# A hybrid decoder layer on one core: cross-attention begun beside its queries, MLP operands by column halves, and the next head's values differenced in a fixed place

## The chip, the core and the metric

The kernel runs on one core of a Trainium2 chip. Five engines work beside each other, each through its own instructions in order: TensorE (PE: matmuls and transposes into PSUM), VectorE (DVE), ScalarE (ACT), GpSimd (POOL) and SyncE (SP, here only issuing DMAs). The metric is the device time in microseconds of one launch.

## The reference

One layer on x of 1024 tokens by 1024 columns, all in float32: a state-space part and stick-breaking attention side by side, an output projection, cross-attention to 256 memory tokens, and an MLP with squared ReLU; then a last RMSNorm. Cut to what the change touches:

```
def stick_breaking_attention(q, k, v):      # 8 heads of 64
    logits = q @ k.T / 8,  mask: s < t
    later = cumsum(log_sigmoid(-logits), from the right) - own
    out[t] = sum_s exp(log_sigmoid(logits) + later)[t, s] * v[s]

def memory_cross_attention(hn, mem, ...):   # 4 heads of 128, 256 memory tokens
    p = softmax(q @ k.T / sqrt(128));  return (p @ v) @ w_o

def sqrelu_mlp(hn, w1, w2):                 # 1024 -> 4096 -> 1024
    return square(relu(hn @ w1)) @ w2

h = x + hybrid_mixer(rmsnorm(x));  h = h + memory_cross_attention(rmsnorm(h), rmsnorm(mem))
h = h + sqrelu_mlp(rmsnorm(h));    out = rmsnorm(h)
```

## The kernel before

Every matmul of float32 operands is done as three (lines 208 to 210), on an upper part (`whi`, rounded by ScalarE) and the rest (`wlo`, a subtraction of VectorE); the helpers `act` (line 107) and `tt` (line 110) record most of ScalarE's and VectorE's work, so the traces are read by tile names. A scheduler orders each engine's instructions by the program's order, by shifts of priority (`later`) and by its own estimates of when an operand is there; the order is then fixed, and each engine waits in it.

**Attention** (`attention`, 230 to 515 us). Per head the values v are loaded twice, shifted by one row (line 710, GpSimd's queue), and their difference is taken on VectorE (`v1`), split and used as the right-hand side of the weighted sum: the sum over s of weights times v is taken over differences of v, so that the running products (the scan of line 739) serve as weights. Per pair of query blocks, m = 0 to 3: logits z (line 736), a sigmoid on ScalarE into `stay`, the scan on VectorE, transposes on TensorE (wT, line 756), the split (wTh, wTl) and the sum into `ops` (line 770). Between them stand matmuls of the projections of the queries and keys (`qkps`; divided by a row factor `rbc` on VectorE) and of the values as filler. The loads and differences of v stand at the head's start, and where the scheduler puts them.

**Cross-attention** (578 to 675 us). `xq(th, a)` makes the queries of head a for half th of the tokens (24 matmuls, `xqps`). `cross` is a unit of one head and one half in two steps: logits `lp`, their maximum and exponentials (`pb`, divided on GpSimd), and then transposes `pT`, their parts `ph` and `pl`, and the sum `avx` with the memory's values. The units are worked one ahead: first step of unit i, second step of unit i-1. Among them stand the last xq and the first four halves of the output product (`xo_half`, `xops`, tables XQ and XF).

**Output and MLP operands** (672 to 732 us). `xo_half(t, n)` makes 512 of the 1024 columns of token tile t (12 matmuls, 2.8 us) and adds them to h on VectorE; `hn` is h times the gain (GpSimd). `rows_T` transposes hn into PSUM (`hT4`, four transposes, line 256, two banks in turn). The MLP's first product is done by a scheme of seven products for a 2 by 2 block, with operands B11, B21 (tokens 0 to 511), B22 and the combinations T1 to T4, each in two parts: with b the transposed half, T1 from t1 = b12 - b11, T2 from t2 = b22 - t1, T3 from t3 = b22 - b12, T4 from r1 = t2 - b21. Before, per token tile, both halves are made and added (`xo_rows`, `gain_rows`) and one tile later transposed and combined (`normB`). VectorE takes the lower part of an operand; `PL` names two operations that GpSimd takes. The first products P1 and P2 of two blocks stand at the end of it, then P6 and P7 begin the MLP proper.

The lines that a scheme can't say, the differences of v in the loop over heads and the order of the units:

```
            tt(v1, v0, v1, ALU.subtract)
            stt(v0[:, 1::2], v0[:, 1::2], B.nlast, v1[:, 1::2], ALU.mult, ALU.add)
...
    for i in range(9):
        for d in range(2):
            if 0 <= i - d < 8:
                next(units[i - d], None)
```

Of the kernel before, what the change touches and what calls it, by code (L numbers as in the profile page):

```python
# [9 lines left out]
F32 = mybir.dt.float32  # L10
# [6 lines left out]
P = 128  # L17
D = 1024
S = 1024
# [4 lines left out]
FF = 4096  # L24
NPR = FF // P // 2
GRP = 8
PL = ('T1', 'R1')
NLAST = 3
E0 = 180
NAHEAD = 2  # L30
# [15 lines left out]
OB = 1  # L46
KKB = 6

XF = (4, 5, 6, 8)
HA0 = 0  # L50
HA1 = 1
LA = 1
# [39 lines left out]
def hybrid_trunk(ctx: ExitStack, tc: tile.TileContext, xT, x, cols, rows, gain, fing, wzd, wp, out):  # L92
# [16 lines left out]
    def tt(out, a, b, op, eng=None):  # L109
        (eng or nc.vector).tensor_tensor(out=out, in0=a, in1=b, op=op)  # L110
# [59 lines left out]
    def split(hi, lo, src):  # L170
        act(hi, src)
        tt(lo, src, hi.bitcast(F32), ALU.subtract)
# [480 lines left out]
    def need(h):  # L653

        ends = {f: 8.0 * (n + 1) for n, f in enumerate(late)}
        return max(ends.get(("qk", h // 2), 0.0), ends.get(("v", h // 4), 0.0), float(N0) if h == 0 else 0.0)
# [41 lines left out]
    nl_ = [0]  # L698

    def attention(heads, B, need=lambda h: 0):  # L700
        for h in heads:
            yield ("need", need(h))
            hh = h % 2

            v0, v1 = (B.p.tile([P, NT, 64], F32, tag=n_, bufs=1, name=n_) for n_ in ("v0", "v1"))
            for o, v in ((1, v0), (0, v1)):
                nc.gpsimd.dma_start(out=v, in_=vd[o:o + S].rearrange("(t p) c -> p t c", p=P)[:, :, 64 * h:64 * h + 64])  # L710
            vt, vl = B.t("vt", [P, NT, P], 2), B.t("vl", [P, 4, P], 2)
            tt(v1, v0, v1, ALU.subtract)
            stt(v0[:, 1::2], v0[:, 1::2], B.nlast, v1[:, 1::2], ALU.mult, ALU.add)
            split(vt[:, :, 0:64], vt[:, :, 64:P], v1)
            split(vl[:, :, 0:64], vl[:, :, 64:P], v0[:, 1::2])
            qs = B.t("qs", [P, S], 2)
            nc.gpsimd.dma_start(out=qs, in_=qd[h])
            ks = []
            for j in range(2):
                ks.append([None, None])  # L720
            for c in range(2):
                for j in range(2):
                    ks[j][c] = B.t("kk", [P, 512], KKB)
                    nc.gpsimd.dma_start(out=ks[j][c], in_=kd[h, 64 * j:64 * j + 128, 512 * c:512 * c + 512])
            opss = {}
            for m in range(4):
                wb = []
                for i in (2 * m, 2 * m + 1):
# [13 lines left out]
                    wb.append(stay)  # L742
                if m % 2 == 0:
                    opss[m // 2] = psum("m1", OB, "ops")
                ops = opss[m // 2]
                oc = 256 * (m % 2)
                for s2_ in range(m + 1):
                    t4 = tr_ps("wT")
                    last = s2_ == m
                    for sb in range(2):  # L750
                        for ii in range(2):
                            if last and sb == 1 and ii == 0:
                                continue
                            o = sb * 256 + ii * P
                            b = 2 * s2_ + sb
                            nc.tensor.transpose(out=t4[:, o:o + P], in_=wb[ii][:, b * P:(b + 1) * P], identity=ident)  # L756
                    with later(-WP):
                        if last:
                            wh, wl = B.wlast[nl_[0] % len(B.wlast)]
                            nl_[0] += 1  # L760
                            for sl in (slice(0, 256), slice(384, 512)):
                                split(wh[:, sl], wl[:, sl], t4[:, sl])
                        else:
                            wh = B.wT("wTh")
                            wl = B.wT("wTl")
                            split(wh, wl, t4)
                    for sb in range(2):
                        v = vl[:, m, :] if last and sb == 1 else vt[:, 2 * s2_ + sb, :]
                        for j, w in enumerate((wh, wl)):
                            nc.tensor.matmul(out=ops[:, oc:oc + 256], lhsT=v, rhs=w[:, sb * 256:sb * 256 + 256],  # L770
                                             start=(s2_ == 0 and sb == 0 and j == 0), stop=(last and sb == 1 and j == 1))
                if m % 2 == 1:
                    od = oT[64 * hh:64 * hh + 64, h // 2, 512 * (m // 2):512 * (m // 2) + 512]
                    act(od, ops[64:128, :], scale=-1.0)
                    tt(od, od, ops[0:64, :], ALU.subtract)
                yield (3.0 + 4.0 * m) / 36.0

    bctx = ExitStack()
# [82 lines left out]
    def calloc(shape, dt, name):  # L861
        return cpl.tile(shape, dt, tag="c", bufs=NC, name=name)
# [123 lines left out]
            mm3(ps, (vm[0][:, mb, a * P:(a + 1) * P], vm[1][:, mb, a * P:(a + 1) * P]), (ph, pl), mb == 0, mb == 1)  # L986
        split(xo[th][:, 0, a, :], xo[th][:, 1, a, :], ps)

    for th in range(2):
        for a in range(2):  # L990
            xq(th, a)
            if th == 0 and a == TL:
                for t in range(NT - LAG1, NT):
                    turn(t)

    xq(0, 2)
    xq(0, 3)
# [15 lines left out]
        ns = slice(512 * n, 512 * n + 512)  # L1013
        tt(h[t][:, ns], ps, h[t][:, ns], ALU.add)

    units = [cross(th, a) for th in range(2) for a in range(4)]
    for i in range(9):
        for d in range(2):
            if 0 <= i - d < 8:
                next(units[i - d], None)  # L1020
        if i in XQ:
            xq(1, 2 + XQ.index(i))
        if i in XF:
            if not wxo:
                wxo.extend(pieces("xo", 0, 4))
            xo_half(XF.index(i), 0)
# [20 lines left out]
    gff = cpl.tile([P, D], F32, name="gff")  # L1047
    nc.scalar.dma_start(out=gff, in_=gain.partition_broadcast(P))

    def gain_rows(t):  # L1050

        hns[t] = []
        for kh in range(2):
            hn = calloc([P, 512], F32, "hn")
            sl = slice(512 * kh, 512 * kh + 512)
            tt(hn, h[t][:, sl], gff[:, sl], ALU.mult, nc.gpsimd)
            hns[t].append(hn)
        nc.sync.dma_start(out=hd[t * P:(t + 1) * P, :], in_=h[t])

    hns = {}  # L1060

    def normB(t):

        th, o = t // 4, (t % 4) * P
        K4 = [P, 4, P]
        for kh in range(2):
            b = rows_T(hns[t][kh])
            if th == 0:
                act(raw[:, kh, :, o:o + P], b)
                splitB(("B11", "B21")[kh], o, b)  # L1070
            elif kh == 0:
                b12, t1 = calloc(K4, F32, "b12"), calloc(K4, F32, "t1")
                tt(t1, b, raw[:, 0, :, o:o + P], ALU.subtract)
                act(b12, b)
                splitB("T1", o, t1)
            else:
                t2, t3 = (calloc(K4, F32, n_) for n_ in ("t2", "t3"))
                tt(t2, b, t1, ALU.subtract)
                tt(t3, b, b12, ALU.subtract)
                splitB("B22", o, b)  # L1080
                r1 = raw[:, 1, :, o:o + P]
                tt(r1, t2, r1, ALU.subtract, nc.gpsimd if "R1" in PL else None)
                splitB("T2", o, t2)
                splitB("T3", o, t3)

    wxo.extend(pieces("xo", len(wxo), 6 - len(wxo)) + pieces("xo", 6, 2, (xop, "woh", "wol", 2)))

    def xo_rows(t):
        for n in range(2):
            xo_half(t, n)  # L1090

    for t in range(4 + LAG):
        xo_rows(t)
        gain_rows(t)
        if t >= LAG:
            normB(t - LAG)
    B["T2"] = hp.tile([P, 2, 4, 512], F32R, tag="h0", name="T2")
    B["T3"] = big(0, [P, 2, 4, 512], F32R, "T3")
    for t in range(4 + LAG, NT):
        xo_rows(t)  # L1100
        gain_rows(t)
        normB(t - LAG)
    for t in range(NT - LAG, NT):
        normB(t)
    B["T4"] = big(1, [P, 2, 4, 512], F32R, "T4")
    for o in range(0, 512, P):
        r1 = raw[:, 1, :, o:o + P]
# [342 lines left out]
```

## Time and profile before

| | |
|---|---|
| median of 3 runs | 1359.4 us (1359.32 to 1359.65) |
| the profiled execution | 1360.99 us, its span 1359.3 us |
| granted TensorE clock, mean | 0.993 |
| weight loads (beside the matmuls) | 1063.8 us, 78% |
| SyncE's queue of DMAs | 155.78 MB, 36.3% of 16 DMA engines |

The profiled execution took 1.6 us more than the median, and its span is 1.7 us shorter than its own time. A granted clock of 1 is 2.4 GHz, 0.5 is 1.2 GHz. Busy times of TensorE hold short waits inside a pipelined row of matmuls, so its idle time is read where it stands ahead of an instruction, in brackets with what released it.

### The profile page before, as it was taken

What the parts mean: (1) busy time and instruction counts of PE and PEld (TensorE: products, weight loads), DVE (VectorE), ACT (ScalarE), POOL (GpSimd) and SP (SyncE); (2) the same over time, 40 slices, a digit from 0 to 9 for tenths busy, and PEclk for the clock granted to TensorE, in tenths of its full rate; (3) what the DMA queues carried; (4) which work ended last, traced back from release to release, by engine and by line L of the source; (5) the groups of instructions that cost most, each with busy time, mean ns of one, the idle gap of its engine ahead of it and who ended that gap; (6) DMA issues with size and microseconds to landing.
All of it is one profiled execution on the core that took longest, in us unless ns stands there. A gap on an engine that the chain in (4) does not pass through costs nothing.

```text
span 1359.3 us, 18383 instructions
## 1 busy us (share of the span) xinstructions
PE 1307.3 (96%) x6469; PEld 1063.8 (78%) x6469; DVE 942.6 (69%) x1523; ACT 701.4 (52%) x1341; POOL 204.3 (15%) x232
## 2 busy tenths in 40 slices
PE   9999999889999899999998999999999999999997
PEld 7989977678767778887786888888887788888885
DVE  7757865586789856546569756665667866589685
ACT  7455542465567633556445545444553585444453
POOL 0000001310211001003363333223330000000000
PEclk9999999899999999999999999999999999999998
DMA  6111345752556524121133554445449943633341
GB/s 219 40 63 47 102 135 138 222 156 67 159 146 203 149 92 132 31 63 32 59 113 124 186 163 138 142 155 163 140 145 331 300 152 93 231 95 95 98 156 70
DMA packets 95852, 181.68 MB, mean 134 GB/s; under 512 B 9808, under 2 KB 14992, under 8 KB 95760
## 3 DMA queue, kind: packets, MB, share of 16 engines
q1 hardware_dynamic: 85040, 155.78, 36.3%
q0 software_dynamic: 8624, 18.88, 5.1%
q10 hardware_dynamic: 2096, 5.84, 1.2%
q8 instruction: 51, 0.84, 0.3%
q14 instruction: 41, 0.34, 0.1%
HBM read 128.00 MB, written 52.46 MB: 133 GB/s over the span
## 4 chain that ended last, share of the span: by engine, by line
PE 78%; DVE 8%; issue 6%; ACT 3%; DMA 3%; POOL 1%; SPq 0%; POOLq 0%; ACTq 0%; DVEq 0%
PE P L208 7%; PE P L210 7%; PE P L209 7%; PE pr L208 7%; PE pr L209 7%; PE pr L210 7%; DVE stay L739 4%; PE o L210 2%; PE o L208 2%; PE o L209 2%; PE ops L770 1%; PE wT L756 1%; DMA wst<-in_wp 1%; PE qkps L208 1%; PE qkps L210 1%
## 5 line engine op out<-in xcount | busy, mean ns | idle before, releaser
L208 PE MATMUL pr<-whi 128*128 128x512 f32 x448 | 175.9, 396 | 3.5 <-ACT whi L107 3.5
L209 PE MATMUL pr<-wlo,whi 128*128 128x512 f32 x448 | 176.8, 395 | 0.2 <-DVE wlo L110 0.2
L210 PE MATMUL pr<-whi,wlo 128*128 128x512 f32 x448 | 176.2, 393 | 0.0
L110 POOL TENSOR_TENSOR c<-c 128x512 f32<-128x512 f32 x60 | 87.1, 1462 | 202.1 <-ACT c L107 199.7
L110 DVE TENSOR_TENSOR wlo<-w1r,whi 128x512 fp32r<-128x512 f32 x92 | 76.9, 838 | 44.3 <-ACT whi L107 44.3
L107 ACT ACTIVATE whi<-w1r 128x512 fp32r<-128x512 f32 x92 | 57.8, 630 | 92.9 <-PE P L209 52.0
L208 PEld LDWEIGHTS pr<-whi 128*128 128x128 f32 x448 | 83.9, 188 | 24.9 <-ACT whi L107 4.4
L208 PE MATMUL P<-T,whi 128*128 128x512 f32 x256 | 101.0, 395 | 0.9 <-ACT p L107 0.6
L210 PE MATMUL P<-T,wlo 128*128 128x512 f32 x256 | 100.7, 394 | 0.0
L209 PE MATMUL P<-T,whi 128*128 128x512 f32 x256 | 100.6, 393 | 0.0
L209 PEld LDWEIGHTS pr<-wlo,whi 128*128 128x128 f32 x448 | 84.2, 188 | 20.4 <-DVE wlo L110 1.2
L210 PEld LDWEIGHTS pr<-whi,wlo 128*128 128x128 f32 x448 | 84.1, 188 | 20.2
L107 ACT ACTIVATE c<-c 128x512 f32<-128x512 f32 x132 | 81.6, 628 | 24.7 <-DVE c L110 23.1
L107 ACT ACTIVATE whi<-wst 128x512 fp32r<-128x512 f32 (+1 forms) x88 | 54.2, 629 | 67.4 <-PE o L210 24.9
L739 DVE TENSOR_TENSOR_SCAN stay<-stay,dg 128x128 f32<-128x128 f32 (+3 forms) x64 | 84.8, 1346 | 3.9 <-ACT stay L107 3.8
L107 ACT ACTIVATE whi<-us 128x512 fp32r<-128x512 f32 x64 | 40.3, 630 | 79.9 <-PE pr L209 67.0
L210 PE MATMUL P<-B,wlo 128*128 128x512 f32 x192 | 76.3, 397 | 0.0
L208 PE MATMUL P<-B,whi 128*128 128x512 f32 x192 | 76.2, 397 | 0.0
L209 PE MATMUL P<-B,whi 128*128 128x512 f32 x192 | 76.1, 396 | 0.0
L110 DVE TENSOR_TENSOR wlo<-wst,whi 128x512 fp32r<-128x512 f32 (+1 forms) x88 | 61.8, 718 | 19.6 <-ACT whi L107 18.3
L110 DVE TENSOR_TENSOR wlo<-us,whi 128x512 fp32r<-128x512 f32 x64 | 44.9, 701 | 34.1 <-ACT whi L107 33.5
L756 PE MATMUL wT<-ident,stay 128*128 128x128 f32 x288 | 51.3, 282 | 16.5 <-DVE stay L739 15.0
(341 smaller groups left out, 3411.1 us busy)
## 6 DMA issues: line engine op xcount, KB each, us to landing
ud<-c SPq DMA_DIRECT2D x112, 256.0 KB, 3.3
wst<-in_wp SPq DMA_DIRECT2D x104, 256.0 KB, 2.8
w1r<-in_wp SPq DMA_DIRECT2D x16, 1024.0 KB, 6.4
us<-ud SPq DMA_DIRECT2D x64, 256.0 KB, 2.7
pair<-in_wp SPq DMA_DIRECT2D x16, 1024.0 KB, 7.7
kk<-kd POOLq DMA_DIRECT2D x32, 256.0 KB, 5.2
p<-ud SPq DMA_DIRECT2D x24, 256.0 KB, 2.6
u<-ud SPq DMA_DIRECT2D x24, 256.0 KB, 2.6
```

The lines of the kernel that those rows point to most:

```text
L107: nc.scalar.activation(out=out, in_=in_, func=func, **kw)
L110: (eng or nc.vector).tensor_tensor(out=out, in0=a, in1=b, op=op)
L208: nc.tensor.matmul(out=ps, lhsT=a[0], rhs=b[0], start=start, stop=False)
L209: nc.tensor.matmul(out=ps, lhsT=a[0], rhs=b[1], start=False, stop=False)
L210: nc.tensor.matmul(out=ps, lhsT=a[1], rhs=b[0], start=False, stop=stop)
L739: nc.vector.tensor_tensor_scan(out=stay[:, 0:W][:, ::-1], data0=stay[:, 0:W][:, ::-1], data1=B.dg1[:, S - W:S][:, ::-1], initial=0.0, op0= ...
L756: nc.tensor.transpose(out=t4[:, o:o + P], in_=wb[ii][:, b * P:(b + 1) * P], identity=ident)
L770: nc.tensor.matmul(out=ops[:, oc:oc + 256], lhsT=v, rhs=w[:, sb * 256:sb * 256 + 256], start=(s2_ == 0 and sb == 0 and j == 0), stop=(last ...
```

## The change

Three parts, in the code and then in the engines' orders. In `attention` the loads of head h+1's values are issued in the second query pair (m == 1) of head h, and the differences are taken in the third (m == 2), with the first of them kept at its place in the program's order; only heads 0 and 7 do both themselves, freely placed. In the cross-attention the first steps of units 0 and 1 stand between the first xq, and the loop runs two units ahead. In the output stage the work goes by column halves: all eight token tiles of columns 0 to 511, then all of 512 to 1023, one half behind; `PL` is empty, so VectorE takes T1's lower part, and t2 is now t3 + b11 from SBUF instead of b22 - t1 from PSUM (r1 stays on GpSimd). XF moves one of the four early output halves by one unit, all weights of xo go through one ring, and h is stored once per token tile when its second half is done.

```diff
-PL = ('T1', 'R1')
+PL = ()
-XF = (4, 5, 6, 8)
+XF = (4, 5, 6, 7)
...
+        def differ_v(h, pinned=True):
+            v0, v1 = vts[h]
             vt, vl = B.t("vt", [P, NT, P], 2), B.t("vl", [P, 4, P], 2)
-            tt(v1, v0, v1, ALU.subtract)
+            ins = nc.vector.tensor_tensor(out=v1, in0=v0, in1=v1, op=ALU.subtract)
+            if pinned:
+                tc.keep_in_program_order(ins)
...
+                if h + 1 in heads:
+                    if m == 1:
+                        yield ("need", need(h + 1))
+                        load_v(h + 1)
+                    elif m == 2:
+                        differ_v(h + 1)
...
+    xq(0, 1)
+    next(units[0])
+    xq(1, 0)
+    next(units[1])
+    xq(1, 1)
...
-    for i in range(9):
-        for d in range(2):
-            if 0 <= i - d < 8:
-                next(units[i - d], None)
+    for i in range(8):
+        next(units[i], None)
+        if i + 2 < 8:
+            next(units[i + 2])
...
+        elif n == 0:
+            b12s[t], t1 = xop.tile(K4, F32, tag="b12", bufs=4, name="b12"), calloc(K4, F32, "t1")
+            tt(t1, b, raw[:, 0, :, o:o + P], ALU.subtract)
+            act(b12s[t], b)
+            splitB("T1", o, t1)
+        else:
+            t2, t3 = (calloc(K4, F32, n_) for n_ in ("t2", "t3"))
+            tt(t3, b, b12s[t], ALU.subtract)
+            splitB("B22", o, b)
+            tt(t2, t3, raw[:, 0, :, o:o + P], ALU.add)
+            splitB("T3", o, t3)
+            splitB("T2", o, t2)
+            r1 = raw[:, 1, :, o:o + P]
+            tt(r1, t2, r1, ALU.subtract, nc.gpsimd)
...
+    seq = [(t, n) for n in range(2) for t in range(NT)]
+    ready = []
+    for t, n in seq:
+        ready.append((t, n, half(t, n)))
+        if len(ready) > LAG:
+            operands(*ready.pop(0))
...
+    for r in ready:
+        operands(*r)
```

VectorE before, at the start of the attention's first head (256 us in the trace): `v1_2601` is the difference of head 1's values, `qkps_2348` a projected block that is divided, `stay` the scans of head 0.

```order
L110 TENSOR_TENSOR ql_2314<-qkps_2315,qh_2313 128x512
L110 TENSOR_TENSOR v1_2601<-v0_2600,v1_2601 128x512
L117 SCALAR_TENSOR_TENSOR v0_2600<-v0_2600,nlast_2250,v1_2601 128x4x64
L110 TENSOR_TENSOR vt_2604<-v1_2601,vt_2604 128x8x64
L110 TENSOR_TENSOR vl_2605<-v0_2600,vl_2605 128x4x64
L110 TENSOR_TENSOR qkps_2348<-qkps_2348,rbc_327 128x512
L739 SCALAR_TENSOR_TENSOR stay_2404<-stay_2404,dg1_2247 128x128
```

VectorE now, the same place and the place to which the difference (`v1_2469`) has gone.

```order
L110 TENSOR_TENSOR ql_2314<-qkps_2315,qh_2313 128x512
L110 TENSOR_TENSOR qkps_2348<-qkps_2348,rbc_327 128x512
L756 SCALAR_TENSOR_TENSOR stay_2404<-stay_2404,dg1_2247 128x128
...
L756 SCALAR_TENSOR_TENSOR stay_2549<-stay_2549,dg1_2247 128x1024
L110 TENSOR_TENSOR wlast01_2253<-wT_2519,wlast00_2252 128x256
L756 SCALAR_TENSOR_TENSOR stay_2622<-stay_2622,dg1_2247 128x128
L756 SCALAR_TENSOR_TENSOR stay_2628<-stay_2628,dg1_2247 128x256
L110 TENSOR_TENSOR wlast01_2253<-wT_2519,wlast00_2252 128x128
L717 TENSOR_TENSOR v1_2469<-v0_2468,v1_2469 128x512
L110 TENSOR_TENSOR wTl_2565<-wT_2559,wTh_2564 128x512
```

Head 1's difference has moved from the front of head 0's first scan to behind head 0's last and the first two scans of head 1 itself; the divided block and the scans move up.

ScalarE before, at the cross-attention's start: `qT` are the split queries, `pb` the exponentials, `ph` the upper part of the transposed weights.

```order
L107 ACTIVATE qT1_5725<-xqps_5856 128x512
L107 ACTIVATE whi_6309<-wst_6307 128x512
L107 ACTIVATE qT0_5724<-xqps_5915 128x512
L107 ACTIVATE qT0_5724<-xqps_5942 128x512
L107 ACT_TABLE_LOAD
L107 ACTIVATE pb_5987,sst_5986<-lp_5979,sst_5986,rxs0_5719 128x256 x2
L107 ACTIVATE pb_6003,sst_6002<-lp_5995,sst_6002,rxs0_5719 128x256 x2
L107 ACTIVATE qT1_5725<-xqps_6011 128x512
L107 ACTIVATE ph_6081<-pT_6070 128x512
```

ScalarE now, at the same place.

```order
L107 ACT_TABLE_LOAD
L107 ACTIVATE pb_5837,sst_5836<-lp_5829,sst_5836,rxs0_5719 128x256 x2
L107 ACTIVATE pb_5853,sst_5852<-lp_5845,sst_5852,rxs0_5719 128x256 x2
L107 ACTIVATE qT1_5725<-xqps_5861 128x512
L107 ACTIVATE whi_5965<-wst_5963,colt_82 128x256 x2
L107 ACTIVATE pb_5896,sst_5895<-lp_5888,sst_5895,rxs0_5719 128x256 x2
L107 ACTIVATE whi_5973<-wst_5971,colt_82 128x256 x2
L107 ACTIVATE pb_5912,sst_5911<-lp_5904,sst_5911,rxs0_5719 128x256 x2
L107 ACTIVATE whi_6394<-wst_6392 128x512
L107 ACTIVATE qT1_5725<-xqps_5920 128x512
```

The table load and the exponentials of two units have moved ahead of the second and third of the remaining queries, and the first `ph` now comes behind all queries but two.

GpSimd before, from the last gain but two (`hn`) to the end of the operands: `raw` is r1, T1 and T4 are lower parts.

```order
L110 TENSOR_TENSOR hn_6889<-h1_4677,gff_6598 128x512
L110 TENSOR_TENSOR raw_6593<-t2_6908,raw_6593 128x4x128
L110 TENSOR_TENSOR T1_6597<-t1_6898,T1_6597 128x4x128
L110 TENSOR_TENSOR hn_6947<-h1_4677,gff_6598 128x512
L110 TENSOR_TENSOR T4_7006<-raw_6593,T4_7006 128x4x128
L110 TENSOR_TENSOR hn_6949<-h1_4677,gff_6598 128x512
L110 TENSOR_TENSOR T4_7006<-raw_6593,T4_7006 128x4x128
L110 TENSOR_TENSOR T1_6597<-t1_6958,T1_6597 128x4x128
```

GpSimd now, in the same stretch.

```order
L110 TENSOR_TENSOR hn_6905<-h1_4677,gff_6598 128x512
L110 TENSOR_TENSOR raw_6593<-t2_6913,raw_6593 128x4x128
L110 TENSOR_TENSOR hn_6938<-h1_4677,gff_6598 128x512
L110 TENSOR_TENSOR T4_7006<-raw_6593,T4_7006 128x4x128
L110 TENSOR_TENSOR raw_6593<-t2_6946,raw_6593 128x4x128
L110 TENSOR_TENSOR T4_7006<-raw_6593,T4_7006 128x4x128
L110 TENSOR_TENSOR hn_6971<-h1_4677,gff_6598 128x512
L110 TENSOR_TENSOR raw_6593<-t2_6979,raw_6593 128x4x128
```

T1 has left GpSimd, and the last gain (`hn_6971`) stands behind two parts of T4 and two r1, where the last gain before (`hn_6949`) stood behind one part of T4.

## Rows read from the trace of the kernel before

**Rows 1.** The page's busy time by engine: us, share of the span, instructions.

```profile
PE 1307.3 (96%) x6469; PEld 1063.8 (78%) x6469; DVE 942.6 (69%) x1523; ACT 701.4 (52%) x1341; POOL 204.3 (15%) x232
```

**Rows 2.** Busy time by window: stretch, length, PE, PEld, DVE, ACT, POOL, clock, DMA share, GB/s.

```profile
251.70:257.00 5.30, 0.01 (x2) 0.01 (x1) 2.84 (x6) 2.64 (x5) 1.02 (x2) 0.91 0.74 242
256.00:262.90 6.90, 5.90 (x17) 4.67 (x18) 5.10 (x10) 4.69 (x10) 1.79 (x2) 0.51 0.60 176
...
630.00:670.00 40.00, 36.42 (x208) 28.95 (x206) 25.51 (x60) 24.64 (x69) 14.43 (x25) 1.00 0.06 16
...
720.20:723.70 3.50, 3.50 (x11) 2.92 (x12) 3.50 (x5) 2.00 (x4) 2.54 (x2) 0.51 1.02 370
```

**Rows 3.** Waits of TensorE, 230 to 515: for what, us in total, times, longest.

```profile
PE wT L756 <- DVE stay L739: 15.0, 31, 0.9
PE z L736 <- ACT stay L107: 7.1, 7, 5.3
```

**Rows 4.** Timeline of VectorE: start, us, instruction, shapes [idle before <-releaser].

```profile
253.60 0.69 DVE L110 TENSOR_TENSOR v<-v,v 128x512 f32<-128x512 f32 x1 [6.61 <-DMA v<-vd]
...
255.94 0.69 DVE L110 TENSOR_TENSOR qkps<-qkps,rbc 128x512 f32<-128x512 f32 x1
```

**Rows 5.** Timeline of GpSimd: the issue of head 1's v.

```profile
246.35 1.80 POOL L710 DMA_DIRECT2D v<-vd  x2 [5.42 <-DVE vt L110]
```

**Rows 6.** Timeline of ScalarE around the first stall.

```profile
245.55 0.58 ACT L107 ACTIVATE qh<-qkps 128x512 fp32r<-128x512 f32 x1
...
255.28 1.28 ACT L107 ACT_TABLE_LOAD   x1
256.58 0.37 ACT L107 ACTIVATE stay<-z,rq 128x128 f32<-128x128 f32 x1
```

**Rows 7.** Timeline of TensorE around the first stall.

```profile
249.21 0.64 PE L736 MATMUL z<-kk,qs 128*128 128x256 f32 x4
...
251.09 0.40 PE L208 MATMUL qkps<-xh,whi 128*128 128x512 f32 x1
251.32 0.39 PE L209 MATMUL qkps<-xl,whi 128*128 128x512 f32 x1
257.00 0.69 PE L736 MATMUL z<-kk,qs 128*128 128x384 f32 x1 [5.29 <-ACT stay L107]
...
258.48 0.63 PE L208 MATMUL qkps<-xh,whi 128*128 128x512 f32 x1
258.91 0.63 PE L209 MATMUL qkps<-xl,whi 128*128 128x512 f32 x1
```

**Rows 8.** Timeline of TensorE at the end of the operands.

```profile
702.23 0.40 PE L208 MATMUL xops<-whi,xo 128*128 128x512 f32 x1
...
720.18 1.04 PE L256 MATMUL hT<-ident,hn 128*128 128x128 f32 x4 [4.47 <-ACT b L107]
...
732.39 0.50 PE L208 MATMUL P<-T,whi 128*128 128x512 f32 x1 [0.62 <-ACT p L107]
```

**Rows 9.** Timeline of VectorE at the end of the operands.

```profile
717.00 1.75 DVE L110 TENSOR_TENSOR s<-w1r 128x512 f32<-128x512 f32 x1
...
719.27 0.67 DVE L110 TENSOR_TENSOR w1r<-w1r 128x512 f32<-128x512 f32 x1
```

**Rows 10.** Timeline of GpSimd at the end of the operands.

```profile
716.49 1.71 POOL L110 TENSOR_TENSOR T<-raw,T 128x512 fp32r<-128x512 f32 x1
```

**Rows 11.** The tile v: its transfers, issue to landing.

```profile
DMA to landing us min/median/max: 3.7/4.3/6.5
```

**Rows 12.** Waits of TensorE, 590 to 670.

```profile
PE avx L208 <- ACT ph L107: 1.4, 3, 0.6
PE pT L980 <- POOL pb L114: 1.0, 2, 0.7
```

**Rows 13.** Groups by form on ScalarE, 620 to 672: count | busy us, mean ns | idle.

```profile
L107 ACT ACTIVATE ph<-pT 128x512 fp32r<-128x512 f32 x16 | 9.3, 601 | 11.3 <-PE pT L980 11.3
```

**Rows 14.** Groups by form on GpSimd, 672 to 699.

```profile
L110 POOL TENSOR_TENSOR hn<-h,gff 128x512 f32<-128x512 f32 x10 | 12.8, 1297 | 16.7 <-DVE h L110 16.7
```

More of the change, by code (lines that the diff above doesn't have):

```diff
@@ L700, in attention, with load_v @@
     def attention(heads, B, need=lambda h: 0):
-        for h in heads:
-            yield ("need", need(h))
-            hh = h % 2
+        vts = {}
+        def load_v(h):
             v0, v1 = (B.p.tile([P, NT, 64], F32, tag=n_, bufs=1, name=n_) for n_ in ("v0", "v1"))
@@ L710, in attention @@
                 nc.gpsimd.dma_start(out=v, in_=vd[o:o + S].rearrange("(t p) c -> p t c", p=P)[:, :, 64 * h:64 * h + 64])
+            vts[h] = v0, v1
+        def differ_v(h, pinned=True):
+            v0, v1 = vts[h]
             vt, vl = B.t("vt", [P, NT, P], 2), B.t("vl", [P, 4, P], 2)
-            tt(v1, v0, v1, ALU.subtract)
+            ins = nc.vector.tensor_tensor(out=v1, in0=v0, in1=v1, op=ALU.subtract)
+            if pinned:
+                tc.keep_in_program_order(ins)
             stt(v0[:, 1::2], v0[:, 1::2], B.nlast, v1[:, 1::2], ALU.mult, ALU.add)
@@ L715, in attention @@
             split(vl[:, :, 0:64], vl[:, :, 64:P], v0[:, 1::2])
+            vts[h] = vt, vl
+        for h in heads:
+            hh = h % 2
+            if h not in vts:
+                yield ("need", need(h))
+                load_v(h)
+                differ_v(h, False)
+            vt, vl = vts.pop(h)
             qs = B.t("qs", [P, S], 2)
@@ L987, in cross @@
         split(xo[th][:, 0, a, :], xo[th][:, 1, a, :], ps)
[L989 to L994, printed above, removed]
+    units = [cross(th, a) for th in range(2) for a in range(4)]
+    xq(0, 0)
+    for t in range(NT - LAG1, NT):
+        turn(t)
+    xq(0, 1)
[3 more added lines that the diff above has]
+    xq(1, 1)
     xq(0, 2)
@@ L1014, in xo_half @@
         tt(h[t][:, ns], ps, h[t][:, ns], ALU.add)
-    units = [cross(th, a) for th in range(2) for a in range(4)]
-    for i in range(9):
-        for d in range(2):
-            if 0 <= i - d < 8:
-                next(units[i - d], None)
+    for i in range(8):
+        next(units[i], None)
+        if i + 2 < 8:
+            next(units[i + 2])
         if i in XQ:
@@ L1048, in hybrid_trunk, with half @@
     nc.scalar.dma_start(out=gff, in_=gain.partition_broadcast(P))
[L1050 to L1062, printed above, removed]
+    def half(t, n):
+        xo_half(t, n)
+        hn = calloc([P, 512], F32, "hn")
+        sl = slice(512 * n, 512 * n + 512)
+        tt(hn, h[t][:, sl], gff[:, sl], ALU.mult, nc.gpsimd)
+        if n == 1:
+            nc.sync.dma_start(out=hd[t * P:(t + 1) * P, :], in_=h[t])
+        return hn
@@ L1064, in normB, with operands @@
+    b12s = {}
+    def operands(t, n, hn):
         th, o = t // 4, (t % 4) * P
         K4 = [P, 4, P]
[L1066 to L1102, printed above, removed]
@@ L1103, in hybrid_trunk @@
-    for t in range(NT - LAG, NT):
-        normB(t)
+        b = rows_T(hn)
+        if th == 0:
+            act(raw[:, n, :, o:o + P], b)
+            splitB(("B11", "B21")[n], o, b)
+        elif n == 0:
[12 more added lines that the diff above has]
+            tt(r1, t2, r1, ALU.subtract, nc.gpsimd)
@@ L1105, in hybrid_trunk @@
+    wxo.extend(pieces("xo", len(wxo), 8 - len(wxo)))
+    seq = [(t, n) for n in range(2) for t in range(NT)]
[4 more added lines that the diff above has]
+            operands(*ready.pop(0))
+        if (t, n) == (4, 1):
+            B["T2"] = hp.tile([P, 2, 4, 512], F32R, tag="h0", name="T2")
+            B["T3"] = big(0, [P, 2, 4, 512], F32R, "T3")
+    for r in ready:
+        operands(*r)
     B["T4"] = big(1, [P, 2, 4, 512], F32R, "T4")
```

## The prediction, made before the changed kernel had run

> **What bounds the kernel now.** I read the page's busy shares first [rows 1]: TensorE is busy 96% of the span of 1359.3 us, so time can come only from the 52 us in which TensorE stands still and from the stretches in which it runs slowly. Next, the busy times by window [rows 2]: the reader is to see that two places hold both. From 251.7 to 257.0 TensorE does nothing, and from 256.0 to 262.9 its granted clock is 0.51, which is the lower of its two levels (1.2 of 2.4 GHz); the same clock stands at 720.2 to 723.7, behind another idle stretch (below). Between 630 and 670 there are 3.6 us of small gaps at full clock. Then the waits of TensorE by releaser in the attention [rows 3]: 15.0 us are 31 waits of at most 0.9 us on the scan, and 5.3 us are one wait. Last, the timelines around both stalls.
>
> The first stall. VectorE stands 6.61 us until a DMA into v has landed [rows 4]: it is the subtraction v1-v0 of head 1 and it starts at 253.60, while its DMA was issued at 246.35 [rows 5]. VectorE works in order, so the division of a query block that comes four instructions later (255.94) and all scans stand behind it. ScalarE is in order too: it splits the new v, which only now is there, loads its table (1.28 us) and only then writes the first sigmoid at 256.58 [rows 6], which lets TensorE go on at 257.00 [rows 7].
>
> The second stall. TensorE ends the products that it has, and the next transposes hT wait 4.47 us for a bank that ScalarE's copy of b gives free [rows 8]. That copy is late because VectorE is: at 717.00 it takes up a difference of two SBUF operands that lasts 1.75 us, while the same operation at 719.27 lasts 0.67 [rows 9]; GpSimd ran one of its own from 716.49 to 718.20 [rows 10], and VectorE's ended 0.55 after it. So, here, a VectorE operation with both inputs in SBUF stands until GpSimd's operation is done.
>
> **The change part by part.** Times are made against the profiled execution, 1360.99 us (span 1359.3 and 1.7 around it); the median of the runs shown is 1359.4, and I take the same difference off it.
>
> *Values of the next head.* Head 1's subtraction leaves its place in front of the query division and stands 28 rows later, behind two scans of head 1; its two DMAs keep their place on GpSimd's queue, behind the keys of the head before. A v transfer took 4.3 us in the median and 6.5 at most [rows 11], so it lands at about 253.5 as before, and VectorE has all of head 0's later scans to do in that time. The 5.29 us wait goes. What is late next is ScalarE's table load and first sigmoid: the table load needs nothing but ScalarE, free at 246.1 [rows 6], and the z of that row ended at 249.85 [rows 7], so sigmoid and scan are done by about 251.5, where TensorE came to its wait at 251.71. I take 5.1 of 5.3. With no long idle stretch ahead of it, the low clock goes too: matmuls of 512 columns follow each other after 0.43 us there and after 0.23 before it [rows 7]; 5.90 us of busy time at 0.51 [rows 2] would be 3.0, a gain of 2.9, less what waits for scans all the same: VectorE is busy 5.1 of those 6.9 us, so I take 2.4. The four VectorE operations on the values (253.60 to 255.94, 2.3 us) [rows 4] and two of ScalarE only change places; in front of head 0's last splits they could cost those 2.3 at the most. The other six heads had their subtraction away from a stall, and their DMAs move one or two places up in GpSimd's queue, past keys that are not urgent; no cost. The 15.0 us of scan waits stay, give or take 2. Sum -7.5, bounds -10.3 (5.3 and 2.9 and 2.1 of small waits) and -2.8 (something else is late at 251.7 and only half of it goes).
>
> *Cross-attention.* The first two logits and exponentials now lie beside xq products, so the softmax of a unit runs two units ahead. The waits named for this stretch are avx on ph (1.4) and pT on pb (1.0) [rows 12]. The second goes: pb has a whole unit more. The first does not: ph is made from a pT that TensorE has just written, some 0.1 for the signal and 0.60 on ScalarE [rows 13], and in the middle units only the next logits lie between. Walking the new order with those durations I find seven such gaps, 0.3 to 1.0 us, some 2.0 in all. Gain 1.6 of 3.6; bounds -3.6 and +1.5 (ScalarE's exponentials in front of a split of the queries).
>
> *Output of the cross-attention and MLP operands.* 16 products, 16 sets of transposes: the same. The lag is one half, 3.2 us of TensorE (a product 2.78, transposes 0.4), not two. An addition of 0.7 (as any of VectorE's) and the GpSimd gain of 1.30 [rows 14] with two signals make 2.2, so the early units go through. The load changes in the last four units, which now hold T2, T3, B22 and T4 together: VectorE does six operations (add, t3, B22 from PSUM; t2, T3, T2 from SBUF) of 0.6, that is 3.6, and GpSimd two of 1.3; T1's lower part has gone to VectorE, earlier. From the end of the fourth-last xops product to P7 it took 732.39 - 702.23 = 30.16 [rows 8], of which 22.4 are products and transposes at full clock. VectorE's operations with two SBUF inputs and all of GpSimd's exclude each other by rows 9 and 10: before 16 x 0.6 + 14 x 1.3 = 27.8, now 20 x 0.6 + 12 x 1.3 = 27.6. So this pair, not TensorE, is the bound of both orders, and the order by halves lightens it by nothing. I walked both orders through all four engines with the spacings of the rows in the tail's timeline (VectorE 0.60, ScalarE 0.52, GpSimd 1.28; the exclusion held for nine tenths of a GpSimd and three quarters of a VectorE operation, which comes nearest to the timeline of before). For before the walk gives 29.8, close to the 30.16; for the new order 30.5: waits of 1.1 (the last hT but one), 3.8 (last hT: its gain stands on GpSimd behind two pieces of T4) and 1.5 (P6), and again about 1.7 of low clock behind the 3.8. So the 4.47 wait does not go, it moves to the last hT: +0.7. Bounds: the wait goes wholly and the clock with it, -6.2; no product covers the pair's excess in the last four units (1.8 + 2.6 against 3.2, 1.2 each), +4.9.
>
> The Trainium skill (SBUF — State Buffer, section Who interferes with whom) says that a VectorE instruction with two SBUF inputs contends with a GpSimd instruction that reads SBUF, and that the one that comes second fully blocks. Rows 9 and 10 agree for the one difference, with its 1.75 against 0.67. Held for whole operations, the same walk gives 31.0 before, more than was measured, and 32.3 now, +1.3 in place of +0.7; without any exclusion it gives 25.1 and 23.6, far from the 30.16, and -1.6. The sum would be 1351.6 by the rule and 1348.7 without it.
>
> Sum: -7.5 - 1.6 + 0.7 = -8.4. The profiled execution would take 1352.6, the median **1351.0**. Smaller edits (xo weights all in one ring, the store of h once per row tile on SyncE) touch transfers that nothing waited for in this stretch; 0.
>
> **Rivals.**
> (a) The pair binds harder in the tail: +4.9 for +0.7, 1355.2. For it: VectorE's 3.6 per unit is over TensorE's 3.2 even alone. Against: P1 and P2 lie behind the last units.
> (b) All goes: 8.2 of the attention, 3.6, and 6.2 of the tail, 1341.4. Against it: the equal load of the pair.
> (c) The attention stall changes its owner at 251.7 (table load, banks of z): only 2.8 comes, 1359.4 - 2.8 - 1.6 + 0.7 = 1355.7. For it: VectorE and ScalarE are both in order, and one is enough to hold TensorE. Against it: no transfer but v's was late there.
> (d) The fixed place makes VectorE stand for a DMA at a later head, since pinned instructions can't give way: 5.3 + 2.4 come back, 1358.7. Against it: issue is one query pair ahead, and 6.5 was the longest landing.
> (e) Slower: the lag of one half is too short. If each addition stands behind a blocked SBUF operation (1.2) and the gain behind another (0.5), the chain is 3.9 against the product's 2.78, 1.15 lost at each of 15 handovers, 17 us: 1368; at half of them 1360 and already no gain. It decides from 0.6 us over the cover per handover. Against it: before the last four units VectorE has only two or three operations per unit.
>
> **How the numbers follow.** A difference under 0.2% (2.7 us) can't be told from none. Forecast 0.49, its own range 1348 to 1354; (a) 0.14; (b) 0.08; (c) 0.10; (d) 0.10; (e) 0.09. Faster: the forecast, (a), (b), (c) less what falls above 1356.7, 0.80; same 0.10, mostly (d); slower 0.10, (e) and a tail of (d). Range 1344 to 1357: it leaves out (b)'s end, half of (d) and (e).
>
> **What would show it.** Right: no TensorE idle over 2 us near 250 and no low clock there; the subtraction of v with no DMA wait over 1 us; 1.5 to 2.5 us of idle time in the cross-attention, nearly all of it avx on ph; a wait of 3 to 5 us at the last hT with low clock behind it, released through GpSimd's hn. Wrong: a stall of over 3 us left in the attention, hT waits spread over the early units, or a tail whose stall is gone.

## The result and the profile after

The changed kernel takes 1353.86 us in the median of 8 runs (1351.84 to 1356.55), against 1359.39 of before in the same session; the ratio of the two is 0.9946, with a 95% interval of 0.9935 to 0.9958. Its profiled execution took 1353.6 us, with a span of 1351.9 and a mean granted clock of 0.997 (0.993 before). It was run again later on another chip, where everything took longer: 0.9955 (0.9941 to 0.9969). The forecast was 1351.0: a gain of 8.4 us, where 5.5 came between the medians and 7.4 between the profiled executions.

To see where the time went, I cut both profiled executions at the same instructions of TensorE (first z; end of the last `ops`; end of the last output projection, `o`; end of the last `xops`; end of the last product `P`, which ends the MLP's first matrix; end of the last `pr`).

| stretch | before | after | difference |
|---|---|---|---|
| start to the first z | 249.21 | 249.83 | +0.6 |
| attention: first z to last `ops` | 263.25 | 258.43 | -4.8 |
| output projection: to last `o` | 65.89 | 65.89 | 0.0 |
| cross-attention and xo: to last `xops` | 133.24 | 131.04 | -2.2 |
| rest of the operands, first MLP matrix: to last `P` | 320.86 | 320.92 | +0.1 |
| second MLP matrix: to last `pr` | 317.33 | 316.28 | -1.1 |

The 9.5 us behind the last `pr` are the same in both.

The first and the last row are not the change's: over all runs of this study the first stretch lies between 249.1 and 250.8 (but for four kernels, below) and the last between 315.8 and 319.1, whatever was changed; the longest wait near its beginning, for a weight piece, lasts from 1.6 to 3.3 us.

The first stall is gone. Busy times by window of the new kernel, with the columns of [rows 2]: the stretches before and behind the last hT, and then the stretch after the first z and the cross-attention.

```profile
711.90:715.90 4.00, 0.02 (x1) 0.00 (x1) 3.84 (x6) 1.72 (x4) 3.21 (x2) 1.00 0.33 131
715.90:719.40 3.50, 3.50 (x11) 2.96 (x12) 3.50 (x5) 1.83 (x4) 1.58 (x2) 0.52 0.46 91
249.80:258.00 8.20, 8.03 (x43) 6.20 (x42) 6.73 (x11) 4.93 (x11) 0.49 (x1) 1.00 1.02 327
...
630.00:670.00 40.00, 38.14 (x214) 30.77 (x213) 24.72 (x53) 23.41 (x59) 14.42 (x21) 1.00 0.17 51
```

After the first z TensorE is busy 8.03 of 8.20 us at full clock where it stood for 5.29 and then ran at 0.51 [rows 2, 7]. In the tail an idle stretch of 4 us with low clock behind it is still there. ScalarE and VectorE at the first place, in their timelines, which stand beside [rows 4, 6]:

```profile
246.94 1.28 ACT L107 ACT_TABLE_LOAD   x1
250.26 0.37 ACT L107 ACTIVATE stay<-z,rq 128x128 f32<-128x128 f32 x1 [2.04 <-PE z L753]
```

```profile
250.03 0.70 DVE L110 TENSOR_TENSOR qkps<-qkps,rbc 128x512 f32<-128x512 f32 x1 [2.38 <-PE qkps L210]
...
271.73 0.68 DVE L717 TENSOR_TENSOR v<-v,v 128x512 f32<-128x512 f32 x1
```

The table is loaded ahead of the first z, the sigmoid waits only for z, and head 1's difference, 18 us later than before, waits for nothing. The waits of TensorE in the attention, beside [rows 3], show what came in place of the stall:

```profile
PE wT L773 <- DVE stay L756: 14.6, 30, 0.9
PE ops L787 <- ACT wTh L107: 3.4, 2, 2.0
PE z L753 <- ACT stay L107: 0.8, 1, 0.8
```

The second row is new: 3.4 us in two waits for wTh, the upper part of the transposed attention weights, at 391.30 and 422.84. The first of them, in the timelines of TensorE, ScalarE, VectorE, SyncE's queue and GpSimd:

```profile
391.30 0.39 PE L787 MATMUL ops<-wTh,vt 128*128 128x256 f32 x1 [1.40 <-ACT wTh L107]
```

```profile
390.13 0.63 ACT L107 ACTIVATE whi<-wst 128x512 fp32r<-128x512 f32 x1 [3.29 <-DMA wst<-in_wp]
390.67 0.58 ACT L107 ACTIVATE wTh<-wT 128x512 fp32r<-128x512 f32 x1
```

```profile
382.19 0.67 DVE L110 TENSOR_TENSOR wlo<-wst,whi 128x512 fp32r<-128x512 f32 x1
```

```profile
382.88 0.33 SPq L191 DMA_DIRECT2D wst<-in_wp  x1
```

```profile
380.70 1.83 POOL L707 DMA_DIRECT2D v<-vd  x2
```

The time to landing of that one transfer, and the stretch of its flight by window, with the columns of [rows 2]:

```profile
DMA to landing us min/median/max: 7.2/7.2/7.2
```

```profile
382.90:390.10 7.20, 6.35 (x38) 4.86 (x36) 4.82 (x6) 2.63 (x5) 1.27 (x3) 1.00 1.08 334
```

The reader is to see the order on ScalarE: the split of a piece of projection weights (`whi`) stands in front of wTh, and it stood 3.29 us until its transfer had landed. That transfer was issued at 382.88, when VectorE had ended the lower part (382.19 to 382.86) of an earlier piece, whose staging buffer was then free. It took 7.2 us, where the median of these transfers is 2.7. The DMA engines were full meanwhile (1.08, 334 GB/s): the two loads of the next head's v, issued from 380.70 on, were under way, and loads of queries and keys with them. So ScalarE, in order, held back wTh, and with it TensorE. In the kernel before a piece at the same place was slow too, 5.5 us from its issue at 392.09, and ScalarE stood for it:

```profile
397.72 0.63 ACT L107 ACTIVATE whi<-wst 128x512 fp32r<-128x512 f32 x1 [1.62 <-DMA wst<-in_wp]
```

But there this split stood behind wTh (395.23) and in front of a smaller copy alone (`wlast`), and TensorE lost 0.65 us to it, at 398.57.

The tail, in TensorE's and GpSimd's timelines, beside [rows 8, 10]:

```profile
706.13 0.66 PE L256 MATMUL hT<-ident,hn 128*128 128x128 f32 x4 [0.94 <-POOL hn L110]
...
715.90 1.12 PE L256 MATMUL hT<-ident,hn 128*128 128x128 f32 x4 [3.98 <-POOL hn L110]
...
726.08 0.50 PE L210 MATMUL P<-T,wlo 128*128 128x512 f32 x1 [1.19 <-DVE wlo L110]
726.41 0.39 PE L208 MATMUL P<-T,whi 128*128 128x512 f32 x1
```

```profile
712.64 1.54 POOL L110 TENSOR_TENSOR T<-raw,T 128x512 fp32r<-128x512 f32 x1 [0.74 <-ACT T L107]
714.13 1.71 POOL L110 TENSOR_TENSOR hn<-h,gff 128x512 f32<-128x512 f32 x1
```

Waits of 0.94, 3.98 and 1.19 us: the prediction's walk had 1.1, 3.8 and 1.5. The multiplication by the gain (`hn`) that the last hT needs begins right behind a piece of T4.

### The profile page after: what moved, and what is told of

The parts are those of the page before. It is cut to its first block, busy times and chain, and to the rows that moved or that the text cites. A ratio compares the mean times of both kernels' runs of the same rounds, so it can differ in the third digit from the quotient of the medians.

```text
span 1351.9 us, 18376 instructions
## 1 busy us (share of the span) xinstructions
PE 1304.6 (97%) x6469; PEld 1062.8 (79%) x6469; DVE 949.1 (70%) x1527; ACT 700.8 (52%) x1341; POOL 199.6 (15%) x228
## 4 chain that ended last, share of the span: by engine, by line
PE 82%; DVE 9%; ACT 3%; DMA 3%; issue 2%; POOL 1%; SPq 0%; POOLq 0%; ACTq 0%; DVEq 0%
PE P L210 7%; PE P L208 7%; PE P L209 7%; PE pr L208 7%; PE pr L209 7%; PE pr L210 7%; DVE stay L756 4%; PE ops L787 2%; PE o L210 2%; PE o L208 2%; PE o L209 2%; PE qkps L208 2%; PE qkps L210 2%; PE qkps L209 2%; PE wT L773 2%
## 5 line engine op out<-in xcount | busy, mean ns | idle before, releaser
L110 DVE TENSOR_TENSOR wlo<-w1r,whi 128x512 fp32r<-128x512 f32 x92 | 81.7, 890 | 40.2 <-ACT whi L107 40.2
L110 DVE TENSOR_TENSOR wlo<-pair,whi 128x512 fp32r<-128x512 f32 x96 | 65.6, 684 | 0.0
```

## The experiments

Ratios are to the kernel before on the same chip, with their 95% intervals. Beside each, "attention", "middle" and "tail" are the table's stretches: first z to last `ops`, last `o` to last `xops`, last `xops` to last `P`; they are 263.25, 133.24 and 320.86 in the kernel before.

| run | ratio | attention | middle | tail |
|---|---|---|---|---|
| attention only | 0.9975 (0.9963 to 0.9987) | 260.4 | 133.4 | 321.1 |
| cross only | 0.9978 (0.9966 to 0.9990) | 264.0 | 130.2 | 321.3 |
| halves only | 1.0008 (0.9993 to 1.0023) | 262.7 | 134.3 | 320.9 |
| no pin | 0.9977 (0.9967 to 0.9986) | 263.6 | 131.3 | 320.9 |
| whole again | 0.9955 (0.9941 to 0.9969) | 259.9 | 131.3 | 320.9 |
| T4 behind the gains | 0.9975 (0.9964 to 0.9986) | 257.1 | 131.3 | 325.8 |
| four staging buffers | 0.9948 (0.9935 to 0.9961) | 254.3 | 131.5 | 321.0 |
| no halves | 0.9946 (0.9933 to 0.9959) | 259.7 | 130.2 | 320.9 |
| late staging | 0.9945 (0.9927 to 0.9962) | 254.7 | 131.1 | 320.9 |
| before, late staging | 1.0022 (1.0011 to 1.0032) | 262.2 | 133.2 | 321.1 |
| five keys | 0.9941 (0.9926 to 0.9956) | 257.6 | 131.2 | 320.9 |
| late staging, no halves | 0.9934 (0.9917 to 0.9951) | 254.5 | 130.0 | 321.1 |

### One part at a time

The three parts of the diff were put into the kernel before, each alone.

Attention only:

> Only the attention part of the change (loads of the next head's values in the second query pair, differences pinned in the third); cross-attention and output stage as before. Theory (the parts act each by itself): the 5.29 us wait near 252 and the low clock behind it are gone, two new waits of 1.4 and 2.0 us near 390 and 420 stand on ScalarE's upper part of a weight piece that has not landed, so about 4.8 us faster than before (ratio 0.9965), and the tail keeps its 4.5 us wait. Rival (the new waits belong to the other parts' order): 7 to 8 us faster and no such waits. Rival (the gain is only the clock's): under 3 us.

Measured 0.9975, 3.4 us where about 4.8 was expected. The old stall is gone and the two new waits are there (1.94 and 1.78 us), so they belong to this part. The first of them in TensorE's timeline, and the stretch behind it by window:

```profile
393.50 0.38 PE L787 MATMUL ops<-wTh,vt 128*128 128x256 f32 x1 [1.94 <-ACT wTh L107]
```

```profile
393.50:397.00 3.50, 3.35 (x13) 2.78 (x14) 3.45 (x8) 1.61 (x5) 0.00 (x0) 0.64 0.66 193
```

Here the granted clock fell to 0.64 for the stretch; in the profile of the whole change a wait of 1.97 us left it at 1.00. So such a wait costs more in one execution than in another.

Cross only:

> Only the cross-attention part (two first steps beside the queries, two units ahead, the fourth early output half one unit sooner). Theory: 2 us faster (1.6 forecast, 2.2 read from the profile of the whole change), ratio 0.9985; the attention's 5.29 us wait and the tail's 4.47 us wait stand as before; avx on ph still waits 1.5 us in all, pT on pb no longer. Rival (what was gained in the cross-attention is lost in a later tail): no change.

0.9978, 3.0 us; the middle is 3.1 us shorter. What is left of TensorE's waits between 590 and 670 in this run, beside [rows 12]:

```profile
PE avx L208 <- ACT ph L107: 1.5, 3, 0.6
```

pT no longer waits for pb, as expected; avx still waits for ph. The gain is more than the idle time that went. TensorE does the same 658 matmuls and transposes between the last `o` and the last `xops` in both kernels, and its idle time there falls from 3.58 to 1.92 us, by 1.7. The rest lies in time that the profile counts as busy: from start to start, against the spacing in an unbroken row (0.23 us for 512 columns, 0.12 for 256, 0.11 for a transpose), the delays add up to 7.7 us before and to 4.8 in this run. The wait for ph that ends at 643.58, for one, is 0.58 us of idle time and puts the next start back by 0.74.

Halves only:

> Only the output stage by column halves with its operand arithmetic. Theory (VectorE's operations with two SBUF inputs and GpSimd's exclude each other, and the pair's work is the same): within 1 us of before; the wait of 4.5 us moves to the last hT, released by GpSimd's gain, with low clock behind it. Rival (the lag of one half is too short): 3 us or more slower with waits of hT on hn in early units. Rival (shorter dependences): 3 us or more faster.

1.0008 with an interval on both sides of 1, so no gain that can be told; middle and tail together are 455.2 against 454.1, 1.1 us longer in the profile, where the walk said 0.7. The wait has moved as forecast, in TensorE's timeline:

```profile
722.62 1.11 PE L256 MATMUL hT<-ident,hn 128*128 128x128 f32 x4 [3.97 <-POOL hn L110]
```

### The place or the earlier loads?

```diff
-        def differ_v(h, pinned=True):
+        def differ_v(h, pinned=False):
```

> The whole change, but the difference of the next head's values is not kept in its place, so the scheduler puts head 1's in front of the divided query block again, as before. Theory (the place on VectorE made the gain in the attention, not the earlier issue of the loads): the wait of about 5 us near 252 is back with the low clock behind it, and the kernel takes 4 to 8 us more than the whole change. Rival (the loads issued a query pair earlier land in time anyway): no wait, time as with the whole change, within 1.5 us.

0.9977 where the whole change has 0.9946 and 0.9955, on other chips, so 3 to 4 us of it are lost, a little less than expected. VectorE and TensorE in the timelines:

```profile
254.10 0.69 DVE L717 TENSOR_TENSOR v<-v,v 128x512 f32<-128x512 f32 x1 [6.82 <-DMA v<-vd]
```

```profile
257.50 0.69 PE L753 MATMUL z<-kk,qs 128*128 128x384 f32 x1 [5.79 <-ACT stay L107]
```

The stall of [rows 4, 7] is back, with a clock of 0.54 in the 6.5 us behind it; the two waits for wTh are not there. Head 1's loads are issued at 246.45, as in the whole change (246.84) and before (246.35); it was the place on VectorE that made the gain.

### The order on GpSimd in the tail

The whole change was run again for comparison, and a version in which T4's lower parts keep their place in the program:

```diff
-        tt(lo, r1, hi.bitcast(F32), ALU.subtract, nc.gpsimd)
+        ins = nc.gpsimd.tensor_tensor(out=lo, in0=r1, in1=hi.bitcast(F32), op=ALU.subtract)
+        tc.keep_in_program_order(ins)
```

> The whole change once more, on the chip of the three runs beside it, to compare them with. Every theory: ratio 0.9946 to before within its interval, 5 to 8 us faster; the last hT waits 4.0 us for GpSimd's gain.

> The whole change, with the four lower parts of T4 on GpSimd kept at their place in the program, so behind the last gain (hn) and all r1; nothing else moves. Theory (the last hT waits because its gain stands on GpSimd behind two T4, and VectorE's operations with two SBUF inputs share the rest): the wait of 4.0 at the last hT falls to 2.4, the one at P6 grows from 1.2 to 2 to 3, 0.6 us faster than the whole change, and up to 2.3 if 2.4 us of idle time leave the clock high, as 2.36 us did at 1056.7 in the trace of before. Rival (the gain waits for its addition on VectorE alone): the last hT waits 4.0 as before and the time is the same.

The whole change again: 0.9955, as expected. The other: 0.9975, not faster but slower, by 2.1 us between the medians. TensorE's timeline:

```profile
712.70 1.11 PE L256 MATMUL hT<-ident,hn 128*128 128x128 f32 x4 [2.41 <-POOL hn L110]
...
723.46 0.50 PE L210 MATMUL P<-T,wlo 128*128 128x512 f32 x1 [1.18 <-DVE wlo L110]
...
726.89 0.79 PE L208 MATMUL P<-T,whi 128*128 128x512 f32 x1 [2.71 <-ACT p L107]
```

The wait of the last hT fell from 3.98 to 2.41, as walked (2.4), so GpSimd's order did set it. What I had wrong is what follows. ScalarE's copy of P1 (p) now stands 6.10 us for GpSimd's last T4 (1.65 in the whole change), in its timeline and GpSimd's:

```profile
726.24 1.08 ACT L107 ACTIVATE p<-P 128x512 f32<-128x512 f32 x2 [6.10 <-POOL T L1128]
```

```profile
719.44 6.78 POOL L1128 TENSOR_TENSOR T<-raw,T 128x512 fp32r<-128x512 f32 x4
```

It needs no operand from there. Its buffer is taken from a pool that begins where the pool with r1 (`raw`) ended, and the last T4 reads `raw`; that it waits for the space is my reading of the code, the row shows only whom it waits for. The clock fell too, and twice (windows of this run):

```profile
712.70:716.20 3.50, 3.50 (x11) 2.98 (x12) 3.50 (x5) 1.82 (x4) 1.28 (x1) 0.53 0.32 78
...
726.90:734.00 7.10, 7.10 (x19) 5.57 (x20) 5.10 (x9) 3.65 (x7) 0.00 (x0) 0.57 0.40 124
```

Behind the waits of 1.18 and 2.71, which stand close to each other, come 7 us of low clock, and the tail is 4.8 us longer. The work of the pair did not shrink: the four T4 in a row take 6.78 us, and the three operations of VectorE beside them that read two SBUF operands 1.75 or 1.76 each. Its waits turned up at another place.

In the run without halves the attention and the cross-attention parts stand with the output stage of before. Expected were the time of the whole change within 1.5 us and the old wait of 4.5 us at the first of the last two hT. It takes 0.9946 and is 1.1 us faster than the whole change on the same chip by the medians; the tail is 320.9 us in both, and the wait is 4.48, released through ScalarE's copy of b. So the order by halves gives nothing.

### The new waits in the attention

```diff
-KKB = 6
+KKB = 5
...
-        if third and nst_[0] % 3 == 0:
-            return third[0].tile([P, 528], F32, tag="wst3", bufs=1, name="wst")
+        if third and nst_[0] % 2 == 0:
+            return third[0].tile([P, 528], F32, tag="wst3", bufs=2, name="wst")
...
-            return self.p.tile([P, 520 if small else S + 8], F32, tag=tag, bufs=n, name=kind)
+            return self.p.tile([P, 512 if small else S + 8], F32, tag=tag, bufs=n, name=kind)
```

> The whole change, with four staging buffers for weight pieces in place of three during the projections and the attention (one key buffer given up for the space). Theory (the two new waits of 1.4 and 2.0 us in the attention are ScalarE standing in order at the upper part of a weight piece whose transfer could only be issued when VectorE had freed a buffer): both fall under 0.5, so 3 us faster than the whole change, more where a wait had lowered the clock, and the times of single executions lie closer together. Rival (the transfers are late for another reason, the queue of SyncE or the load of the DMA engines): the waits stay or move, and the time is within 1 us of the whole change.

The attention takes 254.3 us, 9.0 less than before and 4.1 less than the change alone. All waits of TensorE between 250 and 515 in this run of more than 0.3 us in all, beside the three rows of the whole change above:

```profile
PE wT L773 <- DVE stay L756: 14.7, 29, 0.9
PE ops L787 <- ACT wlast L107: 0.8, 1, 0.8
PE ops L787 <- DVE wlast L110: 0.5, 1, 0.5
PE ops L787 <- DVE wTl L110: 0.5, 2, 0.3
PE z L753 <- ACT stay L107: 0.5, 1, 0.5
```

wTh has gone from the list: the two waits did hang on the staging buffers. The transfers themselves are hardly faster: the piece issued at 387.84 took 5.9 us to land. But no split waits for it. The five times of this run lie between 1355.8 and 1357.3, the six of the whole change on the same chip between 1354.5 and 1358.8, which is too few to call the scatter settled. Yet the ratio is 0.9948, about 1 us faster than the whole change and not 3: the first stage ends at 36.6 in place of 32.8 us, so most of what the attention gave was lost at the start.

Four more runs:

> The whole change with the fourth staging buffer used only from the 31st weight piece on, so not in the first projections, where the run with four buffers throughout lost about 4 us (first stage to 36.6 in place of 32 us). Theory (the waits in the attention belong to the staging buffers): the attention takes 254 us from its first z to its last ops, as with four buffers throughout (254.3), against 258.4 to 259.9 with the change alone and 263.3 before; the first stage ends at 32 to 33; 9 to 11 us faster than before (ratio 0.992 to 0.9935). Rival (the 4 us at the start are the price of the key buffer, or of chance): the first stage ends at 36, ratio as with four buffers throughout, 0.995.

> The kernel before with that same late staging and nothing of the change. Theory (before, the weight pieces were not what the attention waited for; the wait for v was): the 5.29 us wait near 252 stays with its low clock, and the time is within 2 us of before. Rival (the staging is a bound by itself): 3 us or more faster than before.

> Control for the two runs with four staging buffers: the whole change with five key buffers in place of six and nothing else. Theory: within 1.5 us of the whole change, the two waits of 1 to 2.3 us near 390 and 420 stay. Rival (a key that lands later holds z): slower than the whole change by 2 us or more.

> The attention and cross-attention parts with late staging, the output stage as before: what remains if the part that was found worth nothing is left out. Theory: the same time as with it, within 1.5 us, ratio to before 0.992 to 0.9935. Rival (the halves help once the attention no longer waits): 2 us or more slower than with them.

With the fourth buffer used only late (`% (2 if nst_[0] > 30 else 3)`) the attention takes 254.7 us, as expected, but the first stage still ends at 36.9, so that expectation failed: 0.9945. With five keys alone the first stage ends at 32.9, so the key buffer is not the price; of its two waits for wTh one is still at 423.15 (1.68 us), the one near 390 is gone, and another stands at 275.59 (1.01). Both tiles of the tag `wst3` are taken in turn from the start in all versions with the fourth buffer, and this is the difference that is left; it wasn't tried with a tag of its own. TensorE's waits up to 40 us and an issue on SyncE's queue with late staging, and both of the whole change:

```profile
PE first L208 <- ACT xh L107: 4.7, 4, 1.9
```

```profile
2.65 0.43 SPq L191 DMA_DIRECT2D wst<-in_wzd  x1
```

```profile
PE first L209 <- DVE xl L117: 1.4, 2, 0.7
...
PE first L208 <- ACT xh L107: 0.2, 1, 0.2
```

```profile
2.65 1.33 SPq L300 DMA_DIRECT2D xstage<-in_xT  x2
```

With the fourth buffer a weight piece goes out at 2.65 where two tiles of x (`xstage`) went out before, and TensorE then stands for the split of x (`xh`). All runs with that buffer have a weight piece at this place; that it is the cause is read from the queue's order, and no run varied it alone.

In the kernel before, late staging takes 1.0 us from the attention and costs 5.2 at the start (254.4 to the first z): 1.0022, 2.9 us slower, more than the 2 expected at most, and the old stall stays with 5.00 us. So the pieces were not what the old attention waited for. Five keys give 0.9941, no different from the whole change. Late staging without the halves is the best by its number, 0.9934 (0.9917 to 0.9951), but the 0.9946 of the whole change lies in its interval; a version better than the change beyond doubt was not found.

## Why the prediction was right, and where it was not

*Attention, forecast -7.5.* The two steps of it held: the stall and the low clock went, the table load came early enough, and the difference found its data landed. Without the pin both came back, so the cause is shown. The size was off: -4.8 in the profile, -2.8 to -6.1 over the six profiles that hold the change without more staging. The step that failed is "what is late next", with the sentence that gave the moved loads of the other six heads no cost. I looked for the next wait at 251.7 and nowhere else; it was 140 and 170 us further on: a weight piece in flight beside the next head's loads took 7.2 us, ScalarE's split of it stood in front of wTh, and TensorE lost 3.4 us in two such waits and in some executions a low clock behind them. With those waits taken away the attention is 8.6 to 9.0 shorter than before; 1.0 of that late staging gives the kernel before as well, so the part alone is worth 7.5 to 7.9, as forecast. That the piece's split stands in front of wTh could be read from ScalarE's order before the run, and that pieces are slow beside a head's loads from the trace of before (5.5 us at 392.09). How much of the 7.2 us is due to the moved loads of v no run shows.

*Cross-attention, forecast -1.6.* Right in its mechanism (pT on pb goes, avx on ph stays with 1.5 of 1.4) and in the idle time, of which 1.7 went and 1.9 stayed where the walk had 2.0. The term that was too small is the 3.6 that it took for all there was to win: the delays from start to start were 7.7. The part alone gives 3.1, and 2.2 together with the halves, which add about 1 in the same stretch.

*Output stage, forecast +0.7.* Right in size: +1.1 alone, with the waits where the walk put them. From the fourth-last product to P7 it takes 726.41 - 695.40 = 31.0 us (the last three products begin at 695.75, behind a set of transposes) against 30.16. One engine stood for the other here too: VectorE's lower part of a weight that began at 724.26 took 1.76 us and ended 0.55 behind GpSimd's operation of 723.93 to 725.47, as in [rows 9, 10].

*The sum.* -8.4 forecast, -7.4 between the profiled executions (1360.99 to 1353.6). That it comes so near is in part luck: the attention was short by 2.7 and the cross part over by 1.5, and 0.5 comes from the first and the last stretch, which the change does not touch. The profiled execution was 1.6 above the median before and 0.3 below it after; I had assumed the same difference, and this makes 1.9 of the 2.9 us by which the median of 1353.86 misses the 1351.0.

*The rivals.* (d) was the nearest relative of what happened: an in-order engine stood for a DMA at a later head, but it was ScalarE and a piece of weights. (c) did not come: nothing waits at 251.7, where, as it said against itself, no transfer but v's had been late. (a), (b) and (e) did not come: early hT waited for nothing, and the tail neither won nor lost much. In (e) 3.9 less 2.78 is 1.12, not 1.15; its 17 us stay.

## What to carry to other kernels

When a stall is taken out of a stretch, read the order of every in-order engine behind it for instructions that stand in front of the critical one and wait for a DMA: here the next wait was there, 140 us away. When loads are moved, look at what else is in flight at their new place. Where two engines exclude each other, count their common load before and after: here it was the same, a new order only moved the waits, and one operation put later held up another that waited behind it. A pin on one instruction can be worth more than an earlier issue of the transfer that feeds it.

## What was not expected of the hardware

The clock fell after shorter idle stretches than those of [rows 7, 8], and not each time. Read over the 3.5 us behind the wait, it was 0.76 after 1.72 us without the halves (392.71), 0.64 after 1.94 in the attention-only run, 0.59 after 1.99 with late staging (1045.72) and 0.53 after 2.41 with T4 put back. It was 1.00 after 1.97 in the profile of the change (422.84), after 2.28 without the pin (1056.15) and after 2.36, which ended at 1059.08, in that of before. Behind two waits of 1.18 and 2.71 us close to each other it was 0.57 for 7 us, as long a low stretch as behind the old stall of 5.29 us [rows 2].

A transfer of 256 KB that lands in 2.7 us in the median took 7.2 while the DMA engines were full (1.08 in the stretch of its flight), and ScalarE stood 3.29 of them.
